# A hybrid mixer kernel: the first column block in written order, with half of h made before the modulation is complete

## The chip, the cores and the metric

The kernel runs on one core of one Trainium2 chip. The metric is the time of one execution in microseconds (us) of device time. Of the version before the change there are three runs and one profiled execution.

## The reference

The reference is one transformer layer on a sequence of 2048 rows of 1024 float32 values. This is the part that the change touches:

```python
mod = silu(c) @ W_ada + b_ada          # six vectors of 1024: sh1, sc1, gt1, sh2, sc2, gt2
h = rms_norm(x, g_mix) * (1.0 + sc1) + sh1
p = h @ w_in                            # 3088 columns, shared out to the head groups
k_m, i_m, f_m, f_a = ...                # 256 + 16 of these columns are the first block
...
x = x + gt1 * (concat(A, B, C) @ w_out)
x = x + gt2 * conv_ffn(rms_norm(x, g_ffn) * (1.0 + sc2) + sh2)
```

Behind it come three kinds of mixers over the columns of p, an output projection and a convolutional feed-forward network; none of that code changes.

## The kernel before, in words

All matrix products are made three times over (`mm3`, lines 53 to 56): both operands are split into a high part (float32r) and the remainder, and high x high, low x high and high x low go into one PSUM tile. The kernel goes through h in two halves of 1024 rows, and in each half through seven column blocks of `w_in` (`blocks`, lines 1071 to 1079). This case is about what happens before and during block 0 of the first half: 256 columns of k and 16 gate columns, for eight tiles of 128 rows.

Before block 0 can run, the kernel needs

- x: the first four row tiles (`x0`) are loaded (SP queue), squared and summed on ACT (`norm_x`, L531), the sum becomes 1/rms on DVE, POOL (`pow`, L128) and DVE, and DVE scales the tile (L536);
- the modulation: `c` (four KB) is turned by PE and passed through silu on ACT to `cs`; `w_ada` comes in tiles of 128x512 (256 KB). For each of the four column groups n = 0..3 (sh1 and sc1, 512 columns each), `mod_sum` (L431, L433) sums eight tiles on DVE, each times a column of `cs`, and four one-column products on PE (L454) add up the 128 partitions. `first_mod(0)` makes sh1 and sc1 for the first 512 columns (n = 0, 2), `first_mod(1)` for the others (n = 1, 3);
- h itself (`make_h`): PE turns 128x128 pieces of x (L573), ACT scales and shifts (`h32`, L577), DVE rounds to the high part `hh` (L578) and takes the remainder `hl` (L579). k = 0..7 numbers the eight slices of 128 columns of h; k = 0..3 need the first half of the modulation, k = 4..7 the second. tb = 0 is the first 512 rows, tb = 1 the next (`x1` in the change);
- the weights of block 0 (`Weights`): eight tiles, each loaded by two transfers (256 and 16 columns, L598), cast on ACT (L608), remainder on POOL (L609).

Block 0 is then eight results of 8 k x 3 products with 272 columns; each goes out on ACT (L674), and the gate columns on DVE (L676). The weights of block 1 are loaded and split meanwhile (remainder on DVE).

All of this lies outside `tc.manual_schedule()`, which is entered at block 1 (L1114): so a scheduler decides each engine's order up to there, from the code and the data it needs. Setup code (masks, memsets, lines 825 to 869) stands far down in the code and is placed by the scheduler as well. Every engine takes its instructions in the order so fixed. SP issues all DMAs; each transfer waits for the one eight places ahead of it.

## Time and profile before

| | |
|---|---|
| runs of the kernel | 2601.19 us median of 3 (2600.03 to 2602.36) |
| the profiled execution's own time | 2602.76 us, of which its span is 2601.0 us |
| busy in the span | PE 2530.4 us (97%), DVE 2007.6, ACT 1270.6, POOL 397.2 |
| 0 to 30.87 us: up to the first h row on ACT | PE busy 9.52, DVE 21.66, ACT 11.27, POOL 12.30 |
| 30.87 to 47.62 us: up to the first h row of k = 4 | PE 9.19, DVE 14.77, ACT 3.00, POOL 1.63 |
| 47.62 to 78.87 us: up to the first product of block 1 | PE 31.05, DVE 22.74, ACT 20.24, POOL 2.20 |
| 78.87 to 200 us | PE 121.00 of 121.13 |

In rows of the timeline the first number is the start in us from the span's start, the second the duration; then come the engine (PE matmul, PEld weight load, DVE, ACT, POOL, SPq for the issue of a DMA), the line of the code, the operation, what it writes and reads, and how many are merged (x4); in brackets stands how long the engine sat idle before and who released it. [...]

### The profile page before, as it was taken

The numbers are of one execution on the slowest core, as the hardware profiler recorded it, in microseconds if no ns is written. First come the engines' busy times: TensorE is split into PE (matmuls) and PEld (weight loads), VectorE is DVE, ScalarE is ACT, GpSimd is POOL, SyncE is SP. The second block draws the span as 40 slices with busy tenths as digits, with TensorE's granted clock in tenths as the row PEclk, the third lists the DMA queues.
The fourth block names the chain that finished last, engine by engine and source line by source line (L and its number), as shares of the span: only waits on it lengthen the run. The fifth ranks groups of instructions, "written<-read, shape, count | busy, mean of one in ns | idle before, by whom it ended". The sixth has DMA issues, their size and how long they took to land.

```text
span 2601.0 us, 36297 instructions
## 1 busy us (share of the span) xinstructions
PE 2530.4 (97%) x12521; PEld 2095.1 (81%) x12537; DVE 2007.6 (77%) x3433; ACT 1270.6 (49%) x2424; POOL 397.2 (15%) x529
## 2 busy tenths in 40 slices
PE   5999999999999999999999999999999999999999
PEld 4888888878788877778877888888888888788787
DVE  7647666476388889865679888888888887898797
ACT  4333343332388878844455444444444444344443
POOL 2013310133266557510000000000000000000000
PEclk9999999999999999999999999999999999999999
DMA  7345762455564446267823222255222218558533
GB/s 244 108 122 155 210 212 87 127 151 145 174 170 117 135 123 170 53 194 235 283 81 98 81 85 78 89 210 179 84 79 88 83 65 283 174 173 292 182 97 118
DMA packets 302592, 379.58 MB, mean 146 GB/s; under 512 B 31934, under 2 KB 194588, under 8 KB 300360
## 3 DMA queue, kind: packets, MB, share of 16 engines
q1 hardware_dynamic: 302408, 377.26, 46.1%
q8 instruction: 99, 1.62, 0.3%
q14 instruction: 85, 0.70, 0.1%
HBM read 276.44 MB, written 100.74 MB: 145 GB/s over the span
## 4 chain that ended last, share of the span: by engine, by line
PE 42%; DVE 4%; DMA 2%; ACT 1%; issue 1%; SPq 0%; DVEq 0%; ACTq 0%
PE ub L56 10%; PE ub L54 10%; PE ub L55 10%; PE db L55 4%; PE db L56 4%; PE db L54 4%; DMA wd<-in_w_down_dram 1%; DVE wspl L1470 1%; DMA act<-act_d 1%; DVE wspl L1339 0%; DVE t2w L1450 0%; DVE T L1204 0%; DVE yc L1394 0%; ACT yc L1393 0%; DVE o L1512 0%
## 5 line engine op out<-in xcount | busy, mean ns | idle before, releaser
L54 PE MATMUL acc<-wh,hh 128*128 128x512 f32 (+2 forms) x768 | 285.8, 373 | 1.9 <-DVE vhl L775 1.2
L54 PE MATMUL ub<-T,wsph 128*128 128x512 f32 x704 | 276.0, 392 | 6.0 <-ACT wsph L1338 2.4
L55 PE MATMUL ub<-T,wsph 128*128 128x512 f32 x704 | 275.6, 391 | 0.8 <-DVE T L1204 0.4
L56 PE MATMUL ub<-T,wspl 128*128 128x512 f32 x704 | 275.1, 391 | 0.8 <-DVE wspl L1339 0.7
L56 PE MATMUL acc<-wh,hl 128*128 128x512 f32 (+2 forms) x768 | 274.3, 361 | 0.4 <-DVE hl L579 0.4
L55 PE MATMUL acc<-wl,hh 128*128 128x512 f32 (+2 forms) x768 | 274.1, 359 | 0.2
L55 PE MATMUL db<-wspl,wsph 128*128 128x512 f32 x616 | 241.6, 392 | 5.0 <-DVE wspl L1470 4.8
L56 PE MATMUL db<-wsph,wspl 128*128 128x512 f32 x616 | 240.0, 390 | 0.0
L54 PE MATMUL db<-wsph 128*128 128x512 f32 x616 | 239.9, 390 | 0.0
L1338 ACT CAST wsph<-S 128x512 fp32r<-128x512 f32 x176 | 109.4, 623 | 219.7 <-PE ub L55 158.1
L263 DVE TENSOR_TENSOR plo<-tp,phi 128x512 fp32r<-128x512 f32 (+1 forms) x320 | 187.0, 607 | 30.7 <-ACT phi L262 28.5
L54 PE MATMUL ub<-B,wsph 128*128 128x512 f32 x528 | 206.3, 391 | 0.3 <-ACT B L1203 0.3
L55 PE MATMUL ub<-B,wsph 128*128 128x512 f32 x528 | 205.9, 390 | 0.3 <-DVE B L1204 0.3
L56 PE MATMUL ub<-B,wspl 128*128 128x512 f32 x528 | 205.6, 390 | 0.0
L223 ACT ACTIVATE L<-L,nm 128x1024 f32<-128x1024 f32 (+2 forms) x192 | 172.5, 902 | 34.4 <-DVE nm L212 32.4
L259 PE MATMUL tp<-ident,L 128*128 128x128 f32 x1088 | 177.4, 275 | 4.2 <-DVE plo L263 1.7
L262 ACT CAST phi<-tp 128x512 fp32r<-128x512 f32 (+1 forms) x320 | 159.9, 520 | 42.0 <-PE tp L259 40.3
L1469 ACT CAST wsph<-act 128x512 fp32r<-128x512 f32 x132 | 82.3, 623 | 194.5 <-PE db L55 175.5
L206 PE MATMUL sp<-kk,q 128*128 128x512 f32 (+3 forms) x640 | 169.4, 376 | 3.2 <-DVE nm L212 2.2
L228 POOL TENSOR_SCALAR L<-L,rs 128x1024 f32<-128x1024 f32 (+2 forms) x192 | 167.6, 883 | 11.0
L56 PEld LDWEIGHTS acc<-wh,hl 128*128 128x128 f32 x768 | 145.2, 190 | 22.4 <-DVE hl L579 1.2
L54 PEld LDWEIGHTS acc<-wh,hh 128*128 128x128 f32 x768 | 146.3, 191 | 20.5 <-DVE vhl L775 1.4
(323 smaller groups left out, 5915.2 us busy)
## 6 DMA issues: line engine op xcount, KB each, us to landing
w<-in_w_up_dram SPq DMA_DIRECT2D x88, 512.0 KB
...
q<-q_d SPq DMA_DIRECT2D x128, 128.0 KB
...
```

What stands on the lines that cost most here:

```text
L54: T.matmul(ps, lh, rh, start=start, stop=False, skip_group_check=resume)
L55: T.matmul(ps, lh, rl, start=False, stop=False, skip_group_check=resume)
L56: T.matmul(ps, ll, rh, start=False, stop=stop, skip_group_check=resume)
L206: T.matmul(sp[:, b : b + bw], q2[n][:, qs], kk[:, s0 + b : s0 + b + bw], start=n == 0, stop=n == 1 and not last)
L223: A.activation(L[c], L[c], AF.Exp, bias=nm[:, n - 1 : n], scale=-1.0, accum_out=rs[:, c : c + 1])
L228: G.tensor_scalar(t, t, rs[:, 0:1], 1.0, op0=ALU.mult, op1=ALU.mult)
L259: T.transpose(tp[:, i * P : (i + 1) * P], rows[i][j // 8][:, (j % 8) * P : (j % 8 + 1) * P], ident)
L262: A.copy(hi[:, c0:], tp[:, c0:])
L263: V.tensor_tensor(lo[:, c0:], tp[:, c0:], hi[:, c0:].bitcast(F32), op=ALU.subtract)
L1338: A.copy(hi, src)
L1469: A.copy(hi, v)
L1470: V.tensor_tensor(lo, v, hi.bitcast(F32), op=ALU.subtract)
```

## The change

The setup of masks and memsets moves to the front, and the manual schedule begins there, so block 0 with all that leads to it now runs in the order of the code. A new function `first_block` takes the place of `first_mod`, `make_h` for the first 1024 rows, `head_setup` and the eight results of block 0:

- loads are written out in one order; the 16 gate columns of all k come in one transfer (`gw`) and POOL copies them beside the 256 (`L1151` in the new numbering); x1 is loaded into other buffers, two of its tiles in halves;
- the first of the eight `w_ada` tiles of each group goes straight to PE (`column_sum` with a column of `cs`), and DVE sums the other seven;
- k = 0..3 of h for the first 512 rows are made after the first half of the modulation, with the rounding to `hh` on ACT; their products for four results (four PSUM tiles: acc2, mps and two acc) follow while DVE sums the second half;
- k = 4..7 and the rest of these four results follow, then the norm of x1, then the four other results, k by k, with the split of block 1's weights on POOL;
- k results go out as one transfer for four tiles.

The first place is the beginning of SP's queue, where `c`, `x` and the `w_ada` tiles (`wa`) are loaded. Before:

```order
L400 DMA rows<-in_c_dram 8x128
L417 DMA xt<-in_x_dram 128x1024 x4
L423 DMA wa<-in_w_ada_dram 128x512 x3
L423 DMA wa<-in_w_ada_dram 128x512 [waits DMAHW0_49]
L423 DMA wa<-in_w_ada_dram 128x512 [waits DMAHW1_49]
```

Now:

```order
L448 DMA rows<-in_c_dram 8x128 [waits DVE_49]
L465 DMA xt<-in_x_dram 128x1024 x4
L471 DMA wa<-in_w_ada_dram 128x512 x3
L471 DMA wa<-in_w_ada_dram 128x512 [waits DMAHW0_49]
L471 DMA wa<-in_w_ada_dram 128x512 [waits DMAHW1_49]
```

The order of these loads is kept, and the first of them has got a wait for DVE. The tile `rows` lies in the buffer of `m32` (tag tmpA, two buffers), and what it waits for is the last read of `m32`, DVE's thirteenth instruction. These are DVE's first rows now:

```order
L404 MEMSET selb 128x256
L97 CAST identb<-ident 128x128 [waits Pool_49]
L406 CAST selb<-ident 4x512 [waits DVE_49]
L406 CAST selb<-ident 4x512 x2
L409 MEMSET neb_171 128x256
L409 MEMSET neb_172 128x256
L411 MEMSET R 128x512
L419 CAST maskb<-m_181 128x128 [waits Pool_49]
```

Before, maskb's cast stood between two sums of the modulation. The second place is PE's queue at the first products, where `mps<-ones,modacc` is the last sum over partitions of the first half. Before:

```order
L454 MATMUL mps<-ones,modacc 128x1 [waits DVE_49]
L454 MATMUL mps<-ones,modacc 128x1 x3
L573 MATMUL trp<-ident,xt 128x128 [waits Activation_49]
L573 MATMUL trp<-ident,xt 128x128 x3
L573 MATMUL acc<-ident,xt 128x128 [waits Activation_49]
L573 MATMUL acc<-ident,xt 128x128
L573 MATMUL trp<-ident,xt 128x128 [waits Activation_49]
L573 MATMUL trp<-ident,xt 128x128 x3
L573 MATMUL acc<-ident,xt 128x128 x2
L54 MATMUL acc<-wh,hh 128x272 [waits PE_49,Activation_49]
L55 MATMUL acc<-wl,hh 128x272 [waits Pool_49]
L56 MATMUL acc<-wh,hl 128x272 [waits DVE_49]
```

Now:

```order
L490 MATMUL mps<-ones,modacc 128x1 [waits DVE_49]
L490 MATMUL mps<-ones,modacc 128x1 x3
L604 MATMUL trp<-ident,xt 128x128 [waits Activation_49]
L604 MATMUL trp<-ident,xt 128x128 x3
L490 MATMUL mps<-cs,wa 128x1 [waits DMAHW0_49,DVE_49]
L490 MATMUL mps<-cs,wa 128x1 x3
L54 MATMUL acc<-wh,hh 128x272 [waits Activation_49]
L55 MATMUL acc<-wl,hh 128x272 [waits Pool_49]
L56 MATMUL acc<-wh,hl 128x272 [waits DVE_49]
L54 MATMUL mps<-wh,hh 128x272
L55 MATMUL mps<-wl,hh 128x272
L56 MATMUL mps<-wh,hl 128x272
```

There 48 of these products stand ahead of the last sums of the second half; before there were six. The third place is DVE's queue between the last remainder of h for the first 512 rows (`hl`) and the first for the next 512. Before, with the results' gates among the norms (`st`, `xt`):

```order
L579 TENSOR_TENSOR hl<-h_523,hh 128x512 [waits DVE_49]
L532 TENSOR_TENSOR st<-st 128x1 [waits Activation_49]
L534 TENSOR_SCALAR st<-st 128x1 [waits DVE_49]
L676 TENSOR_TENSOR gates<-acc,gbias 128x4x4 [waits DMAHW1_49,DMAHW7_49,DMAHW0_49,Activation_49]
L536 TENSOR_SCALAR xt<-xt,st 128x1024 [waits DMAHW3_49,Pool_49]
L532 TENSOR_TENSOR st<-st 128x1 [waits Activation_49]
L534 TENSOR_SCALAR st<-st 128x1 [waits DVE_49]
L676 TENSOR_TENSOR gates<-acc,gbias 128x4x4 [waits Activation_49]
L536 TENSOR_SCALAR xt<-xt,st 128x1024 [waits DMAHW4_49,Pool_49]
```

Now:

```order
L599 TENSOR_TENSOR hl<-h_650,hh 128x512 [waits DVE_49]
L573 TENSOR_TENSOR st<-st 128x1
L574 TENSOR_SCALAR st<-st 128x1 [waits DVE_49]
L1117 TENSOR_SCALAR xt<-xt,st 128x512 [waits DMAHW3_49,Pool_49]
L1117 TENSOR_SCALAR xt<-xt,st 128x512
L573 TENSOR_TENSOR st<-st 128x1
L574 TENSOR_SCALAR st<-st 128x1 [waits DVE_49]
L1117 TENSOR_SCALAR xt<-xt,st 128x512 [waits DMAHW4_49,Pool_49]
L1117 TENSOR_SCALAR xt<-xt,st 128x512
```

The norms keep their place behind the last `hl`, each tile is scaled in two halves, and the gates have moved behind all of them. On PE all products of the first 512 rows now stand ahead of the first transpose of x1; before, x1's transposes were spread among them (the first stood behind 55 products of 192). From the first product of block 1 on, the rows of all five engines stand in the order they had.

```diff
+    written = ExitStack()
+    written.enter_context(tc.manual_schedule())
+    fc = pool.tile([36, 1], F32, name="fc")
+    V.memset(fc, 0.0)
+    rmask = pool.tile([68, 512], F32, name="rmask")[64:68]
+    selb = pool.tile([P, 4, P], BF16, name="selb")
+    V.memset(selb, 0.0)
+    for r in (32, 64, 96):
+        V.tensor_copy(selb[r : r + 4], bc(ident[r : r + 4, r : r + 4], 2, P))
+    nebs = [pool.tile([P, 512], BF16, name="neb%d" % i, tag="neb") for i in range(2)]
...
+    m32 = pool.tile([P, P], F32, name="m32", tag="tmpA")
+    G.memset(m32, 0.0)
+    G.affine_select(m32, m32, pattern=[[-1, P]], compare_op=ALU.is_ge, fill=NEG, base=0, channel_multiplier=1)
+    V.tensor_copy(maskb, m32)
+    maskT = pool.tile([P, 4, P], BF16, name="maskT")
+    maskf = pool.tile([P, P], F32, name="maskf", tag="tmpA")
...
-    def mod_sum(tiles):
-        acc = pool.tile([P, 512], F32, name="modacc", tag="t2k")
-        for k, st in enumerate(tiles):
-            if k == 0:
-                V.tensor_scalar(acc, st, cs[:, 0:1], None, op0=ALU.mult)
-            else:
-                V.scalar_tensor_tensor(acc, st, cs[:, k : k + 1], acc, op0=ALU.mult, op1=ALU.add)
-        return acc
...
+    V.memset(modp[:, 0:16], 0.0)
+    def column_sum(n, w, col):
+        for j in range(4):
+            T.matmul(
+                modp[:, n * 4 + j : n * 4 + j + 1], w[:, j * P : (j + 1) * P], col,
+                start=False, stop=True, skip_group_check=True,
+            )
...
+    def squares(parts):
+        st = pool.tile([P, 2], F32, name="st", tag="st")
+        for q, t in enumerate(parts):
+            jk = pool.tile([P, 512], F32, name="jk", tag="sq")
+            A.activation(jk, t, AF.Square, accum_out=st[:, q : q + 1])
+        return st
+    def moments(st):
+        V.tensor_tensor(st[:, 0:1], st[:, 0:1], st[:, 1:2], op=ALU.add)
+        V.tensor_scalar(st[:, 0:1], st[:, 0:1], 1.0 / D, EPS, op0=ALU.mult, op1=ALU.add)
+        rsqrt(st[:, 0:1], 1)
+    def halves(xt):
+        return xt[:, 0:512], xt[:, 512:1024]
...
+    def make_part(tb, k, ps, on_scalar=False):
+        h32 = pool.tile([P, TB], F32, name="h32", tag="t2k")
+        hh = pool.tile([P, TB], F32R, name="hh", tag="hT")
+        hl = pool.tile([P, TB], F32R, name="hl", tag="hT")
+        A.activation(h32, ps, AF.Identity, bias=sh1[:, k : k + 1], scale=a1[:, k : k + 1])
+        (A.copy if on_scalar else V.tensor_copy)(hh, h32)
+        V.tensor_tensor(hl, h32, hh.bitcast(F32), op=ALU.subtract)
+        hT[tb, k] = (hh, hl)
+    def turn_part(ps, xs, k, i):
+        t = xs[i] if isinstance(xs[i], tuple) else halves(xs[i])
+        T.transpose(ps[:, i * P : (i + 1) * P], t[k // 4][:, k % 4 * P : (k % 4 + 1) * P], ident)
...
-    written = ExitStack()
-    cur = Weights(blocks[0][0], G, ("q2k",) * 3 + ("qhl",) * 3 + ("wr",) * 2)
-    for k in range(KT):
-        cur.load()
-    for k in range(KT):
-        cur.cast()
-    first_mod(1)
+    def first_block():
+        x0 = [load_x(i) for i in range(4)]
+        ada = {n: list(load_ada(n * 512, "hT")) for n in (0, 2)}
+        r24 = load_rows(g_mix, b_ada[:, 0:2048])
+        cur = Weights(blocks[0][0], G, ("q2k",) * 3 + ("qhl",) * 3 + ("wr",) * 2)
+        gw = pool.tile([P, KT, 16], F32, name="gw", tag="tmpA")
+        dma(gw, w_in[:, C_G : C_G + 16].rearrange("(k p) n -> p k n", p=P))
+        for k in range(KT):
+            cur.load(1)
+        for n in (1, 3):
+            ada[n] = list(load_ada(n * 512, "hT"))
+        dma(gbias[:, 0:8], b_fox_f.broadcast_to([P, 8]))
+        dma(gbias[:, 8:12], b_m_i.broadcast_to([P, 4]))
+        dma(gbias[:, 12:16], b_m_f.broadcast_to([P, 4]))
+        x1 = []
+        for i, tag in enumerate(("t4k", "H", "M1", "sc")):
+            if i < 2:
+                t = pool.tile([P, D], F32, name="xt", tag=tag)
+                dma(t, x[(4 + i) * P : (5 + i) * P, :])
+                x1.append(halves(t))
+            else:
+                t = [pool.tile([P, 512], F32, name="xh", tag=tag) for _ in range(2)]
+                for q in range(2):
+                    dma(t[q], x[(4 + i) * P : (5 + i) * P, q * 512 : q * 512 + 512])
+                x1.append(tuple(t))
+        nx = Weights(blocks[1][0], G)
+        for k in range(4):
+            nx.load()
+        r16 = load_rest()
+        dma(gsgu, g_sgu.broadcast_to([P, 256]))
+        macc = {}
+        def part(n, k):
+            if k == 1:
+                macc[n] = pool.tile([P, 512], F32, name="modacc", tag="t2k")
+                V.tensor_scalar(macc[n], ada[n][1], cs[:, 1:2], None, op0=ALU.mult)
+            else:
+                V.scalar_tensor_tensor(macc[n], ada[n][k], cs[:, k : k + 1], macc[n], op0=ALU.mult, op1=ALU.add)
+        tp = [(tr_ps, acc_ps)[k % 2]() for k in range(4)]
+        def turns0(i):
+            for k in range(4):
+                turn_part(tp[k], x0, k, i)
+        def scale(x, st):
+            V.tensor_scalar(x, x, st[:, 0:1], None, op0=ALU.mult)
+        st = [squares(halves(t)) for t in x0]
+        moments(st[0])
+        moments(st[1])
+        scale(x0[0], st[0])
+        turns0(0)
+        part(0, 1)
+        scale(x0[1], st[1])
+        turns0(1)
+        moments(st[2])
+        column_sum(0, ada[0][0], cs[:, 0:1])
+        part(0, 2)
+        part(0, 3)
+        scale(x0[2], st[2])
+        turns0(2)
+        moments(st[3])
+        part(0, 4)
+        part(0, 5)
+        scale(x0[3], st[3])
+        turns0(3)
+        part(0, 6)
+        part(0, 7)
+        column_sum(2, ada[2][0], cs[:, 0:1])
+        for k in range(1, 4):
+            part(2, k)
+        transposed(colA[:, 0:24], r24, 24)
+        column_sum(0, macc[0], ones[:, 0:1])
+        for k in range(4, 8):
+            part(2, k)
+        column_sum(2, macc[2], ones[:, 0:1])
+        def cast():
+            k = len(cur.tiles)
+            G.tensor_copy(cur.raw[k][:, 256:272], gw[:, k, :])
+            cur.cast()
+        for _ in range(4):
+            cast()
+        first_columns(0)
+        ps = [pp.tile([P, 512], F32, name="acc", tag="acc2"), mps()]
+        def prod(t, tt, k):
+            hh, hl = hT[t, k]
+            o = tt * P
+            mm3(ps[tt][:, 0:272], hh[:, o : o + P], hl[:, o : o + P], *cur.tiles[k], k == 0, k == KT - 1)
+        def turns(x, k):
+            t = tr_ps()
+            for i in range(4):
+                turn_part(t, x, k, i)
+            return t
+        make_part(0, 0, tp[0], True)
+        tp.append(turns(x0, 4))
+        part(1, 1)
+        column_sum(1, ada[1][0], cs[:, 0:1])
+        prod(0, 0, 0)
+        prod(0, 1, 0)
+        make_part(0, 1, tp[1], True)
+        part(1, 2)
+        part(1, 3)
+        prod(0, 0, 1)
+        prod(0, 1, 1)
+        make_part(0, 2, tp[2], True)
+        tp.append(turns(x0, 5))
+        part(1, 4)
+        part(1, 5)
+        prod(0, 0, 2)
+        prod(0, 1, 2)
+        make_part(0, 3, tp[3], True)
+        for _ in range(4):
+            cast()
+        prod(0, 0, 3)
+        prod(0, 1, 3)
+        n_acc[0] += 1
+        for tt in (2, 3):
+            ps.append(acc_ps())
+            for k in range(4):
+                prod(0, tt, k)
+        part(1, 6)
+        part(1, 7)
+        column_sum(3, ada[3][0], cs[:, 0:1])
+        column_sum(1, macc[1], ones[:, 0:1])
+        for k in range(1, 8):
+            part(3, k)
+        column_sum(3, macc[3], ones[:, 0:1])
+        first_columns(1)
+        st = [squares(x1[0])]
+        make_part(0, 4, tp[4])
+        make_part(0, 5, tp[5])
+        st.append(squares(x1[1]))
+        for k in (6, 7):
+            tp.append(turns(x0, k))
+            make_part(0, k, tp[k])
+            for tt in range(4):
+                prod(0, tt, k - 2)
+        for tt in range(4):
+            prod(0, tt, 6)
+            prod(0, tt, 7)
+        def finish(t0):
+            e = pool.tile([P, 4, 256], F32, name="ev4", tag="t4k")
+            for tt in range(4):
+                A.copy(e[:, tt, :], ps[tt][:, 0:256])
+                V.tensor_tensor(
+                    gates[:, 0, :, t0 + tt, :], ps[tt][:, 256:272].rearrange("p (a h) -> p a h", a=4),
+                    gbias.rearrange("p (a h) -> p a h", a=4), op=ALU.add,
+                )
+            dma(km_d[t0 * P : (t0 + 4) * P, :].rearrange("(t p) c -> p t c", p=P), e)
+        for i in range(4):
+            if i > 1:
+                st.append(squares(x1[i]))
+            moments(st[i])
+            for t in x1[i]:
+                scale(t, st[i])
+        tps = [tr_ps(), tr_ps()]
+        for i in range(4):
+            for k in range(2):
+                turn_part(tps[k], x1, k, i)
+        finish(0)
+        ps = [acc_ps(), acc_ps(), acc_ps(), mps()]
+        wsn = pool.tile([P, 4, P], F32, name="wsn", tag="sq")
+        for k in range(KT):
+            make_part(1, k, tps[k], k % 2 == 1)
+            if k + 2 < KT:
+                tps.append(turns(x1, k + 2))
+            nx.cast()
+            nx.load()
+            for tt in range(4):
+                prod(1, tt, k)
+            if k == 3:
+                dma(wsn, w_s[0].rearrange("g t s -> t g s"))
+        finish(4)
+        transposed(colA[:, 24:40], r16, 16)
+        V.tensor_scalar(gq8, colA[:, 32:33], 0.125, None, op0=ALU.mult)
+        for g in range(4):
+            G.affine_select(
+                wsn[:, g, :], wsn[:, g, :], pattern=[[-1, P]], compare_op=ALU.is_ge, fill=0.0,
+                base=0, channel_multiplier=1,
+            )
+        pw = misc_ps()
+        for g in range(4):
+            T.transpose(pw[:, g * P : (g + 1) * P], wsn[:, g, :], ident)
+        A.copy(wT.rearrange("p g t -> p (g t)"), pw)
+        return nx
...
-        if i == 1:
+        if n == nb + 1:
             written.enter_context(tc.manual_schedule())
-        blocks[i][1](half, cur)
+        if n == 0:
+            nxt[0] = first_block()
+        else:
+            blocks[i][1](half, cur)
+            if nxt[0]:
+                nxt[0].cast()
```

## The prediction

> **What bounds the kernel now.** I read the busy time in four stretches first, then the timeline of each engine in the first 80 us. In the table of stretches the columns are the length, then busy us (and count) of PE, PEld, DVE, ACT and POOL, the granted clock, the DMA share and GB/s:

> ```profile
> 0.00:30.87 30.87, 9.52 (x38) 7.63 (x38) 21.66 (x55) 11.27 (x28) 12.30 (x24) 1.00 0.83 278
> 30.87:47.62 16.75, 9.19 (x37) 7.95 (x37) 14.77 (x26) 3.00 (x5) 1.63 (x5) 1.00 0.78 263
> 47.62:78.87 31.25, 31.05 (x222) 29.97 (x223) 22.74 (x55) 20.24 (x44) 2.20 (x4) 1.00 0.45 143
> 78.87:200.00 121.13, 121.00 (x685) 104.92 (x688) 70.99 (x159) 44.10 (x80) 12.36 (x14) 1.00 0.39 115
> ```

> From 78.87 on PE is busy all the time, and the rows of all engines from there on stand in the same order before and after. So the change is worth what it moves block 1's first product, and that shift is carried to the end one for one. Up to 47.62 PE is idle more than half the time: it waits for DVE, which sums the modulation. The three marks that part the stretches are these rows:

> ```profile
> 30.87 0.78 ACT L577 ACTIVATE h<-trp,sh,a 128x512 f32<-128x512 f32 x1 [3.16 <-DVE a L460]
> 47.62 0.78 ACT L577 ACTIVATE h<-trp,sh,a 128x512 f32<-128x512 f32 x1 [5.12 <-DVE a L460]
> 78.87 0.40 PE L54 MATMUL acc<-hh,wh 128*128 128x512 f32 x1
> ```

> The first is h with k = 0, the second h with k = 4; both came when DVE's `a` was there. I take the new kernel from mark to mark.

> **To the first h row (30.87 before).** The new wait is at the very start: SP's first load waits for maskb's cast, and x and all of `w_ada` are queued behind it.

> ```profile
> 0.80 0.41 SPq L400 DMA_DIRECT2D rows<-in_c_dram  x1
> 1.44 0.55 DVE L837 MEMSET neb<- 128x256 uint32 x2
> 1.50 0.29 POOL masks.py:199 TENSOR_SCALAR_AFFINE_SELECT ident<-ident 128x128 f32<-128x128 f32 x1
> 2.04 0.48 DVE L839 MEMSET R<- 128x512 f32 x1
> 7.51 0.22 DVE L97 CAST identb<-ident 128x128 bf16<-128x128 f32 x1
> 8.48 0.42 DVE L834 CAST selb<-ident 4x512 bf16<-4x512 f32 x1
> 23.62 0.22 DVE L847 CAST maskb<-m 128x128 bf16<-128x128 f32 x1
> 15.75 0.29 SPq L400 DMA_DIRECT2D rows<-in_g_mix_dram  x1
> 16.42 0.33 SPq L400 DMA_DIRECT2D rows<-in_b_ada_dram  x1
> ```

> DVE must now wait for ident (1.50 + 0.29 = 1.79), then do identb 0.22, three selb casts 3 x 0.42, neb 0.55, R 0.48 and maskb 0.22: 4.5. So every load starts 3.7 us later than at 0.80. The g_mix load waits for the ninth `w_ada` tile, the next load for the tenth; so the ninth was there at 15.75 at the latest, and one comes each 0.67. DVE's first sum now takes the second tile: 15.75 - 7 x 0.67 = 11.1, plus 3.7, is 14.8. From there DVE works without a pause:

> ```profile
> 19.00 0.48 DVE L431 TENSOR_SCALAR modacc<-wa,cs 128x512 f32<-128x512 f32 x1
> 19.40 4.31 DVE L433 SCALAR_TENSOR_TENSOR modacc<-wa,cs,modacc 128x512 f32<-128x512 f32 x6
> 25.58 2.41 DVE L433 SCALAR_TENSOR_TENSOR modacc<-wa,cs,modacc 128x512 f32<-128x512 f32 x2
> 24.63 6.84 POOL L609 TENSOR_TENSOR wl<-wr,wh 128x272 fp32r<-128x272 f32 x8
> 28.05 1.86 PE L454 MATMUL mps<-ones,modacc 128*128 128x1 f32 x8 [4.43 <-DVE modacc L433]
> ```

> 12 sums at 4.31 / 6 = 0.72 are 8.6, two first products 1.0, three scalings of x at 0.75 (row below) 2.3, four st rows and a copy at 0.16 each 0.8: 12.6, and 27.4. The row at 25.58 shows what comes on top: two sums took 2.41, 1.0 more than 1.44, while POOL split weights. The new order has POOL's first splits there too; I take 0.6: 28.0. Before, the last sum ended at 25.58 + 2.41 = 27.99. So the two sums that PE takes over (0.7 each) and what is moved elsewhere just pay for the late loads: **0.0**, bounds -0.6 and +1.0. POOL's copies of the gate columns are in no row; the nearest row of as few elements is the 0.55 of `st` below, so the four ahead of h are worth 0 to 2.2. I take 0, since they run while DVE sums.

> [...]

> **To h with k = 4 (47.62 before).** ACT now rounds to `hh` too, so DVE has its first remainder after h and one cast:

> ```profile
> 76.43 2.18 ACT L608 CAST wh<-wr 128x512 fp32r<-128x512 f32 x4
> 47.87 0.69 DVE L579 TENSOR_TENSOR hl<-h,hh 128x512 fp32r<-128x512 f32 x1
> 48.48 0.42 DVE L578 CAST hh<-h 128x512 fp32r<-128x512 f32 x1
> 48.94 0.69 DVE L579 TENSOR_TENSOR hl<-h,hh 128x512 fp32r<-128x512 f32 x1
> 43.80 0.74 DVE L433 SCALAR_TENSOR_TENSOR modacc<-wa,cs,modacc 128x512 f32<-128x512 f32 x1
> 44.60 1.87 PE L454 MATMUL mps<-ones,modacc 128*128 128x1 f32 x8
> ```

> 30.9 + 0.78 + 2.18 / 4 and the hand-overs is 32.3; in front of the second half's sums stands this `hl`, so DVE is idle till then, which it was not before. Then 12 x 0.72 + 2 x 0.48 + 4 x 0.61 (47.87 to 48.48) = 12.0, and 1.0 for the splits on POOL beside it: 45.3, against 43.80 + 0.74 = 44.5. The sum over partitions took 1.87, and h came 1.15 after its end. With PE fast again in part (rates below) I take 1.4. That makes 47.9: **+0.3**, bounds -0.8 (no stretching, fast sums) and +2 (PE). PE has to be through its queue by 45.3: from the end of the first h row, 31.7, a turn of 1.1 and a product over partitions of 1.9 stand ahead of the block products, so these begin at 34.7; with another turn, some 17 of them slow and 31 fast (below) they take 0.8 + 17 x 0.23 + 31 x 0.126 = 8.6, and two sums over partitions at 1.0 to 1.9 follow: 45.3 to 47.1. So PE is about as late as DVE, and the 48 products taken early are free only just.

> **To block 1 (78.87 before).** Here is what the change loses. The remainders of k = 4..7, then the four norms of x1 one after the other, with POOL's power in each:

> ```profile
> 5.39 0.61 ACT L531 ACTIVATE jk<-xt 128x512 f32<-128x512 f32 x1
> 55.42 0.16 DVE L532 TENSOR_TENSOR st<-st 128x1 f32<-128x1 f32 x1 [2.61 <-ACT jk L531]
> 55.85 0.55 POOL L128 TENSOR_TENSOR st<-st,nhalf 128x1 f32<-128x1 f32 x1 [8.97 <-DVE st L534]
> 56.44 0.75 DVE L536 TENSOR_SCALAR xt<-xt,st 128x1024 f32<-128x1024 f32 x1 [0.47 <-POOL st L128]
> 57.10 0.15 DVE L532 TENSOR_TENSOR st<-st 128x1 f32<-128x1 f32 x1
> ```

> ACT has two h rows, two squares (0.61 each) and a third h row ahead of k = 6: 3.4; then two k on DVE at 1.07 (47.87 to 48.94): 5.5, 53.4. From st to the scaling is 56.44 - 55.42 = 1.02, and scaling in two halves some 0.8 where one piece let the next start after 0.66: 1.8 a tile, 7.3 for four, 60.7. Before, these norms lay beside products of the same block, and PE did not wait. Now PE has finished the first 512 rows by then: from 47.9, 2.0 to the first remainder, 48 products and two turns at the fast rate are 49.9 + 6.0 + 1.0 = 56.9. The last turn, h and hh add 1.5: 62.2 for the first product of x1. PE's rates:

> ```profile
> 39.05 1.09 PE L573 MATMUL trp<-ident,xt 128*128 128x128 f32 x4
> 52.07 0.43 PE L56 MATMUL acc<-wh,hl 128*128 128x272 f32 x1
> 52.30 0.43 PE L54 MATMUL acc<-wh,hh 128*128 128x272 f32 x1
> 63.55 0.60 PE L573 MATMUL trp<-ident,xt 128*128 128x128 f32 x4
> 77.11 0.29 PE L55 MATMUL acc<-wl,hh 128*128 128x272 f32 x1
> 77.24 0.29 PE L56 MATMUL acc<-wh,hl 128*128 128x272 f32 x1
> 215.07 1.06 PE L1065 MATMUL mps<-ident,hq 128*128 128x128 f32 x8 [2.68 <-DVE hq L1058]
> ```

> Products start 0.23 apart at 52 us and 0.126 apart at 77 us, though the granted clock reads 1.00 in both stretches. So PE was slow for some six us of work behind the sum that ended at 46.5; in the new kernel its dense work begins at 32.8, and I let it be fast from 39 on. Transposes take 1.09 for four early, 0.60 later, and 1.06 for eight after a gap of 2.68 us, so that gap leaves PE fast. 96 products at 0.126 are 12.1, six turns at 0.5 are 3.0: 77.3. The new gap from 56.9 to 62.2 holds only eight transposes, and I take it that PE is slow again after it: some 22 products at 0.1 more, 2.2, as at the first start. 79.5. The two small turns at the end are 1.1: 80.6. **+1.7** in all; without the slow products -0.5.

> [...]

> The other edits cost nothing by these marks: 16-column loads merged into one shorten SP's queue, but DVE, not DMA, is last at both marks; the one k transfer for four tiles is read three blocks later.

> **Sum.** 0.0 + 0.3 + 1.4 = +1.7. The profiled execution took 2602.76, so it would be 2604.5; against the median of the runs, 2601.19, it is 2602.9, rounded to **2603**.

> **Rivals.** [...] Block 1's splits move from DVE to POOL beside x1's products.

> ```profile
> L132 POOL TENSOR_TENSOR wo0l<-ld,wo0h 128x512 fp32r<-128x512 f32 x4 | 5.2, 1296 | 6.6 <-ACT wo0h L131 6.6
> ```

> That row gives 1.30 each, and 6.84 / 8 x 512 / 272 gives 1.61 beside a busy DVE. If they take turns, each k costs 1.61 + 0.69 + half of 0.42 = 2.5, against PE's 12 x 0.126 + 0.5 = 2.0: eight times 0.5 is 3.8, +5.5 and 2606.7; with PE's queue late at k = 4 (+2) it is 2608.7. [...] For it speaks the row at 25.58; against it that PE makes its turns two k ahead. Chance 0.22.

> *The head start counts in full (faster).* 48 products are 6.0 us. If PE did not wait for the norms and stayed fast, 144 products, ten turns, 2.0 and 1.1 make 26.2 from 47.9: 74.1, -4.8, and with the low ends of the first two marks (0.6 and 1.1 less) -6.5: 2594.7. Against it: in the order the norms stand behind the last `hl`. Chance 0.08.

> *The change doesn't act*: the order shows that it does; nothing is left for that.

> **Range and chances.** The forecast's own range is 2599.5 to 2606 (warm or cold, bounds of the first marks), chance 0.70. With part of both rivals the range is 2597 to 2609. A measurement can tell about 0.2%, 5.2 us, from no change: faster 0.08, same 0.70, slower 0.22.

> **What would show it.** SP's first load at 4.5; the first h row at 30 to 32, k = 4 at 47 to 50; DVE's last `xt` scaling at 60 to 62, with PE idle five us before it; products 0.23 apart behind; block 1 at 79 to 83. I am wrong if the norms overlap products, if POOL's 128x512 splits take 1.6 or more and PE waits for `hl` in x1, or if the rows behind block 1 hold more idle time of PE than before.

## The result: 13 us slower, and where they arise

The changed kernel takes 2615.06 us (median of 4 runs, 2614.30 to 2615.36), the kernel before 2601.78 beside it (4 runs, 2600.03 to 2603.63): ratio 1.0042, 95% interval 1.003 to 1.0055. The forecast was 2603 with a range of 2597 to 2609. The profiled execution took 2615.36 with a span of 2613.6, 12.6 more than in the profile before.

The same four stretches in the changed kernel, parted by the same marks (columns as in the prediction):

```profile
0.00:32.40 32.40, 11.47 (x50) 10.33 (x50) 20.76 (x53) 8.39 (x23) 11.30 (x25) 1.00 0.80 271
32.40:50.58 18.18, 14.54 (x88) 14.38 (x88) 14.07 (x21) 8.11 (x16) 6.19 (x8) 0.89 0.97 331
50.58:84.26 33.68, 28.63 (x189) 27.31 (x190) 22.39 (x48) 21.93 (x44) 14.67 (x16) 0.81 0.20 60
84.26:200.00 115.74, 115.46 (x655) 99.94 (x658) 64.90 (x142) 43.69 (x78) 11.33 (x13) 1.00 0.41 122
```

The marks in the changed kernel are these rows, and the last row of the third stretch below:

```profile
32.40 0.78 ACT L597 ACTIVATE h<-trp,sh,a 128x512 f32<-128x512 f32 x1 [0.95 <-DVE a L499]
50.58 0.78 ACT L597 ACTIVATE h<-trp,sh,a 128x512 f32<-128x512 f32 x1 [4.26 <-DVE a L499]
```

Against 30.87, 16.75 and 31.25 the first three are longer by 1.53, 1.43 and 2.43. Block 1 begins 5.39 later, not 1.7; PE is idle 5.05 of the third stretch, and the granted clock is 0.81 there. (The 1.00 of the profile before counts PE's slow start as whole: it is read there although products start 0.227 apart until 53.4 and 0.126 apart behind.) The remaining 7.2 of the 12.6 arise behind block 1, where nothing was changed. From block 1 to the end of the span PE does the same work in both profiles, here before and then now:

```profile
78.87:2601.00 2522.13, 2480.60 (x12228) 2049.56 (x12242) 1948.47 (x3300) 1236.04 (x2349) 381.12 (x497) 1.00 0.46 144
84.26:2613.57 2529.31, 2487.11 (x12229) 2055.24 (x12243) 1946.69 (x3297) 1236.94 (x2349) 381.19 (x497) 1.00 0.46 143
```

PE's idle time there is 42.20 instead of 41.53. What grew is its busy time, by 6.51: the same products took longer.

**The first two stretches.** SP's, PE's and DVE's rows of the changed kernel's timeline:

```profile
5.39 0.41 SPq L448 DMA_DIRECT2D rows<-in_c_dram  x1
14.86 0.49 DVE L1106 TENSOR_SCALAR modacc<-wa,cs 128x512 f32<-128x512 f32 x1 [1.64 <-DMA wa<-in_w_ada_dram]
25.25 0.27 PE L454 MATMUL mp<-ident,rows 24*128 24x24 f32 x1 [1.84 <-DMA rows<-in_b_ada_dram]
25.55 0.18 DVE L457 COPY colA<-mp 128x24 f32<-128x24 f32 x1 [1.40 <-PE mp L454]
25.65 3.87 DVE L1108 SCALAR_TENSOR_TENSOR modacc<-wa,cs,modacc 128x512 f32<-128x512 f32 x4
35.80 1.53 DVE L1108 SCALAR_TENSOR_TENSOR modacc<-wa,cs,modacc 128x512 f32<-128x512 f32 x2
37.85 1.91 DVE L1108 SCALAR_TENSOR_TENSOR modacc<-wa,cs,modacc 128x512 f32<-128x512 f32 x2
40.29 1.92 DVE L1108 SCALAR_TENSOR_TENSOR modacc<-wa,cs,modacc 128x512 f32<-128x512 f32 x2
42.64 5.46 DVE L1108 SCALAR_TENSOR_TENSOR modacc<-wa,cs,modacc 128x512 f32<-128x512 f32 x6
48.16 1.87 PE L490 MATMUL mps<-ones,modacc 128*128 128x1 f32 x8 [2.25 <-DVE modacc L1108]
```

The loads start late as said, and DVE waits for them twice: 1.64 for `wa`, and 1.40 for the copy of the bias row, which the late queue delivers at 25.25 and DVE meets in the middle of its sums. Then four sums take 3.87, 0.97 each, and in the second half the twelve take 10.82, 0.90 each, where I counted 0.72 each and 1.0 more in all. POOL's weight remainders stand beside eight of them; the first two and the last two (1.54 from 46.56 on), with nothing beside them on POOL, took 0.77 each.

**The third stretch.** ACT, DVE, PE and POOL in the changed kernel:

```profile
56.14 0.78 ACT L597 ACTIVATE h<-trp,sh,a 128x512 f32<-128x512 f32 x1 [2.22 <-PE trp L604]
57.41 0.69 DVE L599 TENSOR_TENSOR hl<-h,hh 128x512 fp32r<-128x512 f32 x1
64.44 0.88 DVE L1117 TENSOR_SCALAR xh<-xh,st 128x512 f32<-128x512 f32 x2 [0.66 <-POOL st L128]
64.98 0.69 PE L604 MATMUL trp<-ident,xh 128*128 128x128 f32 x2 [1.36 <-DVE xh L1117]
69.34 1.24 DVE L598 CAST hh<-h 128x512 fp32r<-128x512 f32 x1 [0.20 <-ACT h L597]
70.61 2.37 DVE L599 TENSOR_TENSOR hl<-h,hh 128x512 fp32r<-128x512 f32 x2
72.86 2.72 POOL L641 TENSOR_TENSOR wl<-wr,wh 128x512 fp32r<-128x512 f32 x2 [1.14 <-ACT wh L640]
84.26 0.48 PE L54 MATMUL acc<-hh,wh 128*128 128x512 f32 x1
```

The norms of x1 stand behind the last `hl` as forecast and take 1.8 each, but from 58.0 on, and the last scaling comes at 64.44 instead of 60 to 62; PE waits for them as said. Beside POOL's splits of block 1 (1.28 to 1.62 each) DVE's work for x1 is stretched, `hl` to 1.0 to 1.2 instead of 0.69 and a cast to 1.24 instead of 0.43, but PE shows no wait for `hl`.

**The clock.** The granted clock of the changed kernel, in stretches of 3.41 us:

```profile
43.09:46.50 3.41, 2.82 (x26) 2.73 (x24) 3.30 (x4) 1.66 (x5) 2.36 (x3) 1.00 1.03 396
46.50:49.92 3.42, 1.76 (x8) 1.76 (x8) 1.53 (x3) 0.00 (x0) 0.00 (x0) 0.50 0.94 300
53.33:56.74 3.41, 3.41 (x17) 3.41 (x17) 1.40 (x3) 1.19 (x2) 0.00 (x0) 0.50 0.08 24
56.74:60.16 3.42, 3.42 (x29) 3.42 (x28) 2.44 (x8) 3.15 (x11) 0.55 (x1) 1.00 0.00 0
60.16:63.57 3.41, 1.85 (x13) 1.18 (x11) 2.04 (x8) 0.75 (x2) 1.10 (x2) 1.00 0.39 138
63.57:66.98 3.41, 1.39 (x6) 0.95 (x6) 2.02 (x10) 1.49 (x3) 0.68 (x2) 0.50 0.05 16
66.98:70.40 3.42, 3.42 (x18) 3.42 (x17) 2.54 (x3) 2.81 (x5) 3.31 (x3) 0.50 0.16 43
```

It falls to half at 46.50 and 63.57 and is whole again at 56.74 and 70.40, each time after one stretch that PE filled: the first of these holds 17 of PE's instructions at half clock, the next stretch 29. All borders are 3.413 us apart or a multiple of that. So are those far behind block 1: from the fall at 46.50 to the one at 2244.70 it is 2198.2 us, 644 times 3.4133. The profile before and the changed kernel around the first place where PE waits 2.7 us for `hq`, in the same stretches:

```profile
210.36:213.77 3.41, 2.03 (x9) 1.31 (x7) 2.87 (x7) 1.66 (x4) 2.67 (x3) 1.00 0.70 207
213.77:217.18 3.41, 2.11 (x14) 1.93 (x15) 3.34 (x8) 0.62 (x1) 1.04 (x2) 1.00 0.67 237
```

```profile
217.18:220.60 3.42, 0.87 (x4) 0.38 (x2) 2.88 (x6) 2.22 (x5) 2.42 (x3) 1.00 0.87 272
220.60:224.01 3.41, 3.26 (x12) 3.00 (x13) 2.83 (x8) 0.00 (x0) 0.90 (x1) 0.50 0.31 112
224.01:227.42 3.41, 3.41 (x16) 2.80 (x16) 3.34 (x10) 0.60 (x1) 1.44 (x1) 1.00 0.09 35
```

```profile
220.75 1.94 PE L1051 MATMUL mps<-ident,hq 128*128 128x128 f32 x8 [2.70 <-DVE hq L1044]
```

The wait is the same (2.68 in the row at 215.07 before, 2.70 here). Before, it lies across a border, each stretch keeps 2.0 us of work, and the clock stays. 5.7 us later it lies within one stretch that keeps 0.87, and the next runs at half clock. Read off in steps of 0.05 us, the clock falls in the changed kernel at 46.50, 63.60, 220.60, 384.45, 555.10, 1347.00, 1360.65 and 2244.70, each time a whole number of periods behind the others; in the profile before once, at 1336.75 (the last 1.5 us of each span left aside). Comparing ACT's and DVE's rows, which stand in the same order, the changed kernel is behind by 5.7 at 200 us, 7.2 at 230, 8.2 at 392, 10.1 at 600, 10.6 at 1250, 11.6 at 1320, 12.8 at 2300. Three falls (220, 384, 555) thus stand for 1.5, 0.8 and 1.6 by their place.

### The profile page after: what moved, and what is told of

Read it like the earlier page. It is cut to its first block, busy times and chain, and to the rows that moved or that the text cites. A ratio compares the mean times of both kernels' runs of the same rounds, so it can differ in the third digit from the quotient of the medians.

```text
span 2613.6 us, 36358 instructions
## 1 busy us (share of the span) xinstructions
PE 2541.8 (97%) x12553; PEld 2107.3 (81%) x12569; DVE 2003.9 (77%) x3418; ACT 1275.4 (49%) x2431; POOL 413.4 (16%) x545
## 3 DMA queue, kind: packets, MB, share of 16 engines
q8 instruction: 99, 1.62, 0.3%
## 4 chain that ended last, share of the span: by engine, by line
PE 76%; DVE 9%; DMA 7%; ACT 3%; issue 3%; POOL 1%; SPq 1%; ACTq 0%; DVEq 0%; POOLq 0%
PE ub L56 10%; PE ub L54 10%; PE ub L55 10%; PE acc L54 6%; PE acc L55 6%; PE acc L56 5%; PE db L55 4%; PE db L56 4%; PE db L54 4%; PE sp L206 3%; PE tp L259 3%; PE op L245 2%; PE op L246 2%; DMA wd<-in_w_down_dram 1%; DVE L L212 1%
## 5 line engine op out<-in xcount | busy, mean ns | idle before, releaser
L54 PE MATMUL acc<-wh,hh 128*128 128x512 f32 (+2 forms) x752 | 282.9, 377 | 1.2 <-DVE vhl L807 1.2
L54 PE MATMUL ub<-T,wsph 128*128 128x512 f32 x704 | 276.4, 393 | 5.9 <-ACT wsph L1516 2.4
L55 PE MATMUL ub<-T,wsph 128*128 128x512 f32 x704 | 276.2, 392 | 0.5 <-DVE T L1382 0.5
L56 PE MATMUL ub<-T,wspl 128*128 128x512 f32 x704 | 275.9, 392 | 0.8 <-DVE wspl L1517 0.7
L55 PE MATMUL acc<-wl,hh 128*128 128x512 f32 (+2 forms) x752 | 270.7, 361 | 0.2
L56 PE MATMUL acc<-wh,hl 128*128 128x512 f32 (+2 forms) x752 | 270.4, 361 | 0.0
L55 PE MATMUL db<-wspl,wsph 128*128 128x512 f32 x616 | 241.1, 392 | 5.5 <-DVE wspl L1648 5.4
L56 PE MATMUL db<-wsph,wspl 128*128 128x512 f32 x616 | 240.2, 390 | 0.0
L54 PE MATMUL db<-wsph 128*128 128x512 f32 x616 | 240.2, 390 | 0.0
L54 PE MATMUL ub<-B,wsph 128*128 128x512 f32 x528 | 205.7, 390 | 0.0
L55 PE MATMUL ub<-B,wsph 128*128 128x512 f32 x528 | 205.4, 389 | 0.0
L56 PE MATMUL ub<-B,wspl 128*128 128x512 f32 x528 | 205.3, 389 | 0.0
L223 ACT ACTIVATE L<-L,nm 128x1024 f32<-128x1024 f32 (+2 forms) x192 | 172.5, 902 | 34.2 <-DVE nm L212 32.3
L1647 ACT CAST wsph<-act 128x512 fp32r<-128x512 f32 x132 | 82.3, 623 | 195.6 <-PE db L55 176.1
L54 PEld LDWEIGHTS ub<-T,wsph 128*128 128x128 f32 x704 | 133.3, 189 | 37.5 <-ACT wsph L1516 6.5
L56 PEld LDWEIGHTS acc<-wh,hl 128*128 128x128 f32 x752 | 143.1, 191 | 21.4
```

Of the source, the lines that this page charges most:

```text
L54: T.matmul(ps, lh, rh, start=start, stop=False, skip_group_check=resume)
L55: T.matmul(ps, lh, rl, start=False, stop=False, skip_group_check=resume)
L56: T.matmul(ps, ll, rh, start=False, stop=stop, skip_group_check=resume)
L223: A.activation(L[c], L[c], AF.Exp, bias=nm[:, n - 1 : n], scale=-1.0, accum_out=rs[:, c : c + 1])
L1647: A.copy(hi, v)
```

## The experiments

Theory G: a grid of 3.413 us decides on PE's clock, so an unchanged wait costs 1.6 us or nothing by where it lies. Against it theory O: the 7.2 us come from the change's code. In the first block three causes stood side by side: L, the late loads; N, x1's norms; P, POOL's reads beside DVE.

### Delays at block 1 (e1 to e4, e9)

```diff
+                while n_dup[0]:
+                    n_dup[0] -= 1
+                    T.matmul(ps, wh[:, 0:P], hh, start=True, stop=True)
                 mm3(ps, wh[:, j * P : (j + 1) * P], wl[:, j * P : (j + 1) * P], hh, hl, k == 0, k == KT - 1)
```

Kernel before, 24 repeats. 

> The kernel before, with block 1's first product issued 24 times more ahead of itself (each restarts its sum, so the result is unchanged): 24 x 0.227 = 5.45 us of extra PE work, and block 1's real work starts at 84.3, where the changed kernel starts it (84.26). Theory G (a fixed grid of 3.413 us, beginning 2.15 us into the span: a stretch of it in which PE worked less than about half is followed by a stretch at half clock): sliding the grid over the PE gaps of the kernel before gives new falls of the granted clock at 220.6, 384.4 and 555.1, as in the changed kernel, and a time 10.6 to 10.7 above the kernel before: 2612 to 2613. Theory O (the 7.2 us that the changed kernel loses behind block 1 come from something in its code, such as the later loads or POOL's work): only the extra work shows, +5.4, about 2607, and the granted clock stays 1.00 at 220, 384 and 555.

Measured: 2613.34 (5 runs), ratio 1.0034 (1.0022 to 1.0047). The stretch with `hq`'s wait and the next, in this kernel:

```profile
217.23:220.64 3.41, 0.72 (x4) 0.30 (x3) 2.87 (x6) 1.98 (x5) 2.17 (x2) 1.00 0.97 314
220.64:224.05 3.41, 3.41 (x13) 3.02 (x14) 2.80 (x9) 0.00 (x0) 0.90 (x1) 0.50 0.19 71
```

These are the changed kernel's rows, without a line of its code: theory O falls for this place. The falls at 384.4 and 555.1 did not come, others at 1033 and 1347 to 1361 did, so the list of falls was right only in part; the time was right.

Kernel before, 10 repeats. 

> The same with 10 repeats, 10 x 0.227 = 2.27 us. Theory G: falls of the granted clock near 217.2, 381 and 551.7, and +7.3 to +7.4 over the kernel before, about 2609. Theory O: +2.3, about 2604.

Measured: 2610.47 (9 runs), 1.0027 (1.0017 to 1.0036), with falls at 217.00, 380.80 and 551.50. As G said.

Kernel before, 15 repeats. 

> The same with 15 repeats, 15 x 0.227 = 3.41 us, one whole period of the supposed grid. Theory G: every gap lies in the grid as in the kernel before, so no fall at 217, 381 or 552, and +3.4 only, about 2605: less than with 10 repeats, although more work is added. Theory O: +3.4 as well, and more than with 10 repeats.

Measured: 2609.86 (11 runs), 1.0024 (1.0015 to 1.0032), with falls at 217.75 and 548.85. A miss: one period of delay did not bring the kernel back.

Changed kernel, 6 repeats. 

> The changed kernel with block 1's first product issued 6 times more, 1.36 us: its start moves from 84.26 to 85.62, two periods of the grid (6.83) behind the start of the kernel before, 78.87. Theory G: the falls at 220.6, 384.4 and 555.1 go, and the time is about that of the kernel before plus 6.8: 2608.5, some 6 us less than the changed kernel although work is added. Theory O: 1.4 more than the changed kernel, 2616.5.

Measured: 2613.39 (5 runs, 2612.14 to 2616.19), ratio 1.0037 (1.0023 to 1.0051), with a fall at 222.45 in the profile. A miss as well: the median is 1.7 below the changed kernel's although work was added, and not 6, and the runs of the two overlap, so this run does not decide between G and O. For the two profiled executions the borders show why the waits did not lie where I had put them: in e3 they stand 2.71 us behind a multiple of 3.413 from the span's start, in e4 0.58, in the changed kernel and the kernel before 2.13 and 2.16. The grid does not start with the program. In the 17 profiles of this study 8 lie between 1.8 and 2.2 and the rest anywhere from 0.3 to 3.2. Where it lay in the other executions, which make the medians, is not known.

Kernel before, one repeat. 

> The kernel before with block 1's first product issued once more, 0.23 us. It asks whether the 3 to 5 us that each of the delays of 10, 15 and 24 repeats lost beyond its own length come from the delay or from an added instruction as such. Theory G (position of the gaps in the grid): 0.23 us moves no gap across a border that matters, so 0 to +1 over the kernel before. Theory C (any added instruction shifts the code behind it, and the engines wait for instructions): +3 to +5, as with the longer delays.

Measured: 2604.49 (11 runs) against 2602.98, ratio 1.0002 (0.9992 to 1.0011): at most 2.9 for one more instruction. Theory C, with its 3 to 5, falls, if narrowly. In the profile the clock falls at 215.4 all the same, as the borders of this execution stand 0.34 behind a multiple.

### The waits filled (e13, e14)

```diff
             yp = mps()
+            for n in range(9 if j == 0 and qi in (0, 2) else 0):
+                T.matmul(yp, identb, selb.rearrange("p r c -> p (r c)"), start=True, stop=True)
             for n in range(4):
                 T.transpose(yp[:, n * P : (n + 1) * P], hq2[:, n, j * P : (j + 1) * P], ident)
```

In the kernel before. 

> The kernel before with nine products of 512 columns in each of the two places where PE stands still 2.7 us for hq. Theory G: the kernel before mostly sits so in the grid that these gaps lie across a border and cost nothing; filling them gives 0 to 1.5 us less on the median, and no fall near 215 and 548 in the trace. Rival (falls there come in it as often as in the others): 2.5 to 3 us less.

Measured: 2604.12 (11 runs) against 2602.34, ratio 1.0006 (0.9998 to 1.0015): nothing gained, and no fall near 215 or 548.

In the changed kernel. 

> The changed kernel with the same filling. Theory G: its falls at 220.6 and 555 go, 1.6 us each, in nearly all executions: 2.5 to 3.5 us less, 2611.5 to 2612.5; the falls near 384, 1347 and 2245 are not touched. Rival (the 7.2 us behind block 1 don't hang on the clock): no change within 1 us, 2614 to 2616.

Measured: 2610.54 (6 runs), 1.0033 (1.002 to 1.0045): 4.5 less than the changed kernel, and every run (2606.47 to 2612.37) below every run of that (2614.30 to 2615.36). PE's rows at the first place, and the stretches there:

```profile
217.51 2.12 PE L1051 MATMUL mps<-selb,identb 128*128 128x512 bf16 x9
220.27 1.09 PE L1053 MATMUL mps<-ident,hq 128*128 128x128 f32 x8 [0.65 <-DVE hq L1044]
```

```profile
216.15:219.56 3.41, 3.41 (x16) 1.72 (x14) 2.87 (x6) 2.03 (x5) 2.67 (x3) 1.00 0.69 206
219.56:222.98 3.42, 2.77 (x17) 2.40 (x17) 3.12 (x7) 0.25 (x1) 1.05 (x2) 1.00 0.53 190
```

No fall there or near 555 any more. This profile alone would not show it, as its borders stand 1.11 behind a multiple and the fall near 384 is gone too, where nothing was filled; the runs do. Above the kernel before of its own session the median is 8.2 instead of 13.3, a larger gain than forecast, though the intervals of the two ratios overlap. Useless work in PE's idle time is worth 4.5 us in the one kernel and nothing in the other: the loss behind block 1 is in good part the clock, which the kernel before then mostly escapes.

### The first block's causes one by one (e5 to e8, e10, e15)

Masks in buffers of their own (the same for `maskf`):

```diff
-    m32 = pool.tile([P, P], F32, name="m32", tag="tmpA")
+    m32 = pool.tile([P, P], F32, name="m32", tag="kT")
```

> The changed kernel with the two masks of the setup in buffers of their own, so that SP's first load no longer waits for DVE's maskb cast. Theory L (the late loads set the first h row): first load at 0.8 instead of 5.39, DVE's first sum at 11 instead of 14.86, no wait for the b_ada row, the first h row at 28 to 29.5 instead of 32.40, and block 1 3 to 4.5 us earlier (80 to 81.5). Rival W (DVE's own work sets it): the first h row within 0.7 us of 32.40.

Measured: 2608.34 (10 runs), 1.0019 (1.001 to 1.0028). First load at 0.81, and of this kernel's timeline:

```profile
10.87 0.49 DVE L1106 TENSOR_SCALAR modacc<-wa,cs 128x512 f32<-128x512 f32 x1 [1.41 <-DMA wa<-in_w_ada_dram]
21.36 0.18 DVE L457 COPY colA<-mp 128x24 f32<-128x24 f32 x1 [1.18 <-PE mp L454]
28.20 0.78 ACT L597 ACTIVATE h<-trp,sh,a 128x512 f32<-128x512 f32 x1 [0.95 <-DVE a L499]
80.38 0.48 PE L54 MATMUL acc<-hh,wh 128*128 128x512 f32 x1
```

As L said but for the b_ada row, for which DVE still waits 1.18: that wait comes from the row's place in the queue and only 0.2 of it from the late start. Without the late start block 1 comes 3.9 us earlier and the median is 6.7 lower. The new order is 2.7 faster than the old one to the first h row, so what I took for an even trade was a gain that the buffer ate.

x1's norms moved ahead:

```diff
+        st = [squares(t) for t in x1]
+        for t in st:
+            moments(t)
         first_columns(1)
...
+            scale1(k - 5)
...
+        make_part(1, 0, tps[0])
         for tt in range(4):
             prod(0, tt, 6)
             prod(0, tt, 7)
-        for i in range(4):
...
```

> The changed kernel with the squares, moments and scalings of x1 moved ahead (squares before h with k = 4, scalings between the remainders of k = 4 to 7), and x1's first turns and first h ahead of the last 24 products. Theory N (the four norms behind the last remainder are what PE waits for from 61 to 67, and that wait is what takes its clock away at 63.6): no gap and no fall there, and block 1 at 76.5 to 78.5 instead of 84.26, 6 to 8 us less in all. Rival Q (DVE's and ACT's queues are full, so the wait only moves to the products of k = 6 and 7): block 1 at 81 or later.

Measured: 2609.58 (9 runs), 1.0023 (1.0014 to 1.0033); no gap and no fall ahead of x1, but block 1 at 81.37, 2.9 earlier instead of 6 to 8. N is right on the wait, but its forecast was too large. From its first turn behind h with k = 4 on, PE is idle 2.15 us here and 4.22 in the changed kernel, and 1.12 of the 2.15 are two new waits for `hl` (0.21 and 0.91). PE and DVE in this kernel, then DVE in the kernel in which block 1's remainders are taken from POOL as well:

```profile
67.85 3.35 DVE L599 TENSOR_TENSOR hl<-h,hh 128x512 fp32r<-128x512 f32 x2
69.56 0.39 PE L56 MATMUL acc<-wh,hl 128*128 128x272 f32 x1 [0.91 <-DVE hl L599]
81.37 0.48 PE L54 MATMUL acc<-hh,wh 128*128 128x512 f32 x1
```

```profile
67.36 0.69 DVE L599 TENSOR_TENSOR hl<-h,hh 128x512 fp32r<-128x512 f32 x1
69.03 0.69 DVE L599 TENSOR_TENSOR hl<-h,hh 128x512 fp32r<-128x512 f32 x1
78.61 0.48 PE L54 MATMUL acc<-hh,wh 128*128 128x512 f32 x1
```

```diff
-        nx = Weights(blocks[1][0], G)
+        nx = Weights(blocks[1][0])
```

> The kernel with x1's norms moved ahead, and with block 1's weight remainders on DVE instead of POOL. Theory P (POOL's reads of SBUF stretch DVE's remainders of x1, 1.3 to 1.7 instead of 0.69 each): hl at 0.69 to 0.75 throughout x1, PE's waits for hl (0.21 and 0.91) go, block 1 at 80 to 80.5 instead of 81.37. Rival V: eight remainders of 0.69 more on DVE make DVE the bound of x1, and block 1 comes at 82 or later.

One execution, 2611.94. `hl` goes from 1.67 to 0.69 and PE's wait of 0.91 is gone: P. (The one of 0.21 stays.) Block 1 came earlier than said, but in this execution the clock was whole 3.3 us sooner after its first fall (54.40, not 57.65), so the 2.8 between the two are not all P's.

Splits of k = 4 to 7 behind the sums:

```diff
         make_part(0, 3, tp[3], True)
-        for _ in range(4):
-            cast()
...
         column_sum(3, macc[3], ones[:, 0:1])
+        for _ in range(4):
+            cast()
         first_columns(1)
```

> The changed kernel with the rounding and POOL's remainders of the weight tiles k = 4 to 7 issued behind the second half's sums instead of beside them. Theory P (POOL's SBUF reads stretch DVE's sums, as in the pair that took 2.41 in the kernel before): the last eight sums of the first stretch and the twelve of the second take 0.73 each instead of 0.77 to 0.96, the second half's sums end 1.9 us earlier (46.2 instead of 48.10) and h with k = 4 comes at 48.5 to 49. Rival: the sums stay at 0.9 each beside SP's loads, so the cause is the DMA writes, and nothing moves by more than 0.4.

Measured: 2615.27 (4 runs), block 1 at 83.96. A failed experiment: the casts were only written further down, and as neither ACT nor POOL has anything else in its queue there, no engine's order changed. It is a second look at the changed kernel, no more.

All three edits, where the casts do come later, behind the first squares of x1 on ACT. 

> The three edits together. If L, N and P are right, they add up but for the order of the queues: h with k = 4 at 45 to 46.5, block 1 at 71 to 74, that is 5 to 8 us ahead of the kernel before (78.87), and the time 2596 to 2604, the width being the falls of the clock behind block 1. If one of the rivals is right, block 1 stays behind 76.

Measured: 2608.72 (11 runs), 1.002 (1.0012 to 1.0029), block 1 at 78.80: a miss. The last six sums took 4.69 instead of 5.46, but ACT had the four casts, each 1.42 behind POOL's, ahead of h with k = 4, and PE waited 5.33 for it. The gain of the late splits was lost in a queue.

The clock kept up around the sums, nothing else:

```diff
         column_sum(3, ada[3][0], cs[:, 0:1])
+        warm(6)
         column_sum(1, macc[1], ones[:, 0:1])
+        warm(6)
...
         column_sum(3, macc[3], ones[:, 0:1])
+        warm(6)
```

> The changed kernel with 18 extra products of 512 columns into an unused bank, six behind each of the last three sums over partitions that PE makes, where it otherwise has little to do. Theory G: no fall of the clock at 46.5, so the last sum takes 1.0 instead of 1.87 and the products of k = 4 and 5 start 0.126 apart instead of 0.227. But the norms of x1 still come when DVE has made them, so PE only waits longer for them: block 1 moves by 0.5 to 2 us (82.3 to 83.8), and the fall in the gap ahead of x1 stays. Rival (PE's slow products are the bound up to x1): block 1 at 80 or earlier.

Measured: 2612.66 (5 runs), 1.0034 (1.0022 to 1.0047), block 1 at 83.06, 1.2 earlier, and the fall ahead of x1 stays (65.40). The last sum took 0.95 instead of 1.87. As G said: PE's slow clock is not the bound here, the norms are.

### A version without the losses (e11, e12)

The early load, the norms ahead, block 1's remainders on DVE, the extra products, and POOL's remainders behind its powers:

```diff
+        for k in range(4):
+            A.copy(hi[k], cur.raw[4 + k])
...
+        st = [squares(t) for t in x1]
+        moments(st[0])
+        moments(st[1])
+        for k in range(4):
...
+            G.tensor_tensor(lo, cur.raw[4 + k], hi[k].bitcast(F32), op=ALU.subtract)
         first_columns(1)
```

> The changed kernel with the early first load, x1's norms ahead, block 1's remainders on DVE, POOL's remainders of k = 4 to 7 held behind its powers for x1 (behind DVE's sums in effect), and twelve extra products of 512 columns into an unused bank around the sums over partitions, which keep the clock up. Theory G: PE's matmul work decides each stretch of the grid, so the fall that the other versions show 3 us ahead of the second half's columns goes, the sum over partitions takes 1.0 instead of 1.87, the products behind h with k = 4 start 0.126 apart, and block 1 comes at 71 to 73.5. Rival: the sums over partitions or the queue behind them are late by the extra products, or the clock falls all the same; block 1 at 75 or later. Time 2599 to 2606 if the part behind block 1 costs 3 to 6 us more than in the kernel before's shown execution, as in all runs so far.

Measured: 2602.76 (11 runs), ratio 0.9997 (0.9988 to 1.0006). Of its timeline:

```profile
37.23 4.69 DVE L1108 SCALAR_TENSOR_TENSOR modacc<-wa,cs,modacc 128x512 f32<-128x512 f32 x6
43.33 3.13 POOL L1215 TENSOR_TENSOR wl<-wr,wh 128x272 fp32r<-128x272 f32 x4
73.59 0.48 PE L54 MATMUL acc<-hh,wh 128*128 128x512 f32 x1
```

With POOL behind them the last ten sums take 1.53 + 1.53 + 4.69 = 7.75 instead of 9.29, and block 1 starts 5.3 us ahead of the kernel before: the change's head start is real once its three costs are gone. But the median is level with the kernel before: the 5.3 are lost behind block 1. In the profiled execution, 2600.36, 2.4 of them are left at the end.

With `hq`'s two waits filled as above. 

> The same, with nine products of 512 columns (2.0 us) into the bank that waits for the transposes of hq, in the two places where PE stands still for 2.7 us for DVE (215 and 545 us in the kernel before). Theory G: with those gaps filled no stretch of the grid falls below half there, whatever its phase, so no fall of the clock near 215 and 548, and 1 to 3 us less on the median than the version without. Rival: the clock falls for another reason than the gaps: falls there all the same, and no gain.

Measured: 2600.21 (11 runs) against 2602.98, ratio 0.9991 (0.9983 to 1.0): 2.8 less than the kernel before, at the edge of what can be told. No fall near 215 or 548; its lead of 4.8 at 90 us is still 4.5 at 1100 and 3.2 at the end.

## Why the prediction was wrong

- **"That shift is carried to the end one for one"** is the step that failed most: 5.39 became 12.6. The same order of instructions did not take the same time: a wait of 2.68 across a border left the clock at 1.00, one of 2.70 within a stretch was followed by 3.41 us at 0.50, and the borders' place against the span differed between executions (2.13 in the changed kernel, 2.71 in e3, 0.58 in e4). The fast rate was in my terms, but only as something inside block 0; I asked for PE's gaps behind block 1 only whether there would be more, and named more idle time as the sign; it grew by 0.7, the busy time by 6.5. I quoted the row at 215.07 and concluded "that gap leaves PE fast": true of that execution, since the wait lay across a border.
- **To the first h row (0.0 forecast, +1.53 measured).** The wait for maskb was found and its size nearly right (5.39 for 4.5). Missed were the 1.40 behind the bias row (1.18 of it also with the early start, e5), and that the sums slow down to 0.97 beside POOL: four of them took 1.0 more than at 0.72, where 0.6 was taken in all. That PE's two sums and the rest "just pay for the late loads" was wrong as well: without the late start the new order is 2.7 faster (e5). The bound of +1.0 was too tight.
- **To k = 4 (+0.3 forecast, +1.43 more measured).** The term that was too small is the 1.0 for POOL's splits beside the twelve sums: these took 10.82 instead of 12 x 0.72 = 8.6, so 2.2. In e11, without POOL beside them, they took 0.78 each. The last sum over partitions took 1.87, the upper end that I had named, where I had taken 1.4.
- **To block 1 (+1.4 forecast, +2.43 measured).** The gap of some five us ahead of x1 and the products 0.227 apart behind it came as said (61 to 67, until 70.4). Its place was 5 us later: the clock had also fallen at 46.5, during the sums over partitions, which I had counted as work that keeps PE fast. So the turn for k = 7 stood behind slow products and the norms began at 58.0. The 2.2 for 22 slow products behind the gap is an estimate that no run shows; in the changed kernel twelve products stand 0.227 apart there (67.09 to 69.73), which is 1.2 us more than at 0.126.
- **The rivals.** The slower one named a real cost that did not decide here: POOL's splits stretch `hl` in x1, but PE does not wait for it, and h follows every 1.94 us per k on ACT (70.82 to 78.60 for four), not every 2.5. That POOL and DVE take turns there was assumed; no run shows it. With the norms moved ahead `hl` takes 1.67 and PE waits 0.91 for it; its price of 3.8 (eight times 0.5 would be 4.0) isn't confirmed, as e6 and e10 differ by 2.8 with a part of the clock in it. Its total of 2608.7 was too low because the tail was missing. That the early products count in full was wrong for this kernel; its 74.1 is reached by e11 (73.59), which has five other edits besides.
- **The range** ended at 2609. No case in it held a loss behind block 1, and that alone is 7.2; without it the execution would have ended near 2608.2, inside the range.

Not settled: three falls stand for 3.9 of the 7.2 us behind block 1. Of the other 3.3, some 2.3 arise at 1250 to 1320 and 2180 to 2300, where executions differ by 2 to 3 us without any fall, DVE waiting longer for the transfers of x (14.8 us from 1240 to 1330 in the changed kernel, 12.6 in the kernel before) or for the w_down tiles from DRAM (9.1 and 7.1 from 2180 to 2310; e8 loses 2.7 at the latter). The changed kernel's fall at 2244.70 is not their cause: DVE's row at 2242.32, ahead of it, is already 12.9 late. What makes those waits longer is open. And if the grid lay anywhere with the same chance, a pure delay would cost its own length on the median; 10, 15 and 24 repeats cost 3 to 5 us more. That the grid prefers one place, as half of the profiles suggest, would explain it, but the timed runs do not show where it lay.
